# A state-space layer's vector work: GpSimd operations moved to VectorE or dropped, the lag matrix spread by DMA, one scan per unit, and the gated output fetched back from DRAM

## The chip, the cores and the metric

The kernel runs on one NeuronCore of a Trainium2 chip. The metric is the device time of one execution in microseconds; the number given for a kernel is the median of its runs, and lower is better. The engines are named as in the profile: PE is TensorE (PEld its weight loads), DVE is VectorE, ACT is ScalarE, POOL is GpSimd, SP is SyncE, which issues nearly all transfers here.

## The reference, cut to what matters

One inference step of a two-layer decoder: 1024 prompt tokens and 64 sample tokens (8 sequences of 8), width 1024. The change lies in the first mixer, a diagonal complex state-space layer (S5), and in the start of the gated linear unit behind it:

```python
lam_bar = exp(lam * dt)                       # 64 groups x 64 complex states
bu  = einsum('blgc,gpc->blgp', u, b_bar)      # 16 channels of a group -> 64 states
h   = pows * h_prev + associative_scan(lam_bar, bu)
y   = real(einsum('blgp,gcp->blgc', h, c)) + d_skip * u
z   = gelu(y)
gl  = z @ w_glu                               # 1024 -> 2048
out = gl[..., :1024] * sigmoid(gl[..., 1024:])
```

Everything is float32. Then follow a convolutional feed-forward layer, differential attention and a second feed-forward layer, which the change leaves as they are.

## The kernel before, in words

The kernel is written against a tile framework with a scheduler: the program is recorded in the order of the code, and the scheduler (`tile.TileContext(nc, schedule_with_timeline_sim=True)`) then sets the order of instructions on each engine. An engine runs its instructions strictly in that order, and so does SP's queue of DMA issues. Tiles come from pools with a fixed number of buffers per name; an instruction that writes a buffer waits until the readers of its last contents are done.

`s5()` handles 1024 tokens as 128 chunks of 8 steps (`NCH`=128, `L`=8). Inside a chunk the recurrence is a matrix product over 8 x 16 = 128 (step, channel) pairs; between chunks it is a scan along 128 chunk numbers. The 64 groups go in 8 blocks of 8 (`BG`=8), and each block in units of 3, 3 and 2 groups: 24 units.

For each block there are
- `angles(b)`: the tables `cosT`, `sinT` (128 x 1024) of the chunk rotation, by two POOL operations (L416, L419), one on DVE (L417) and four on ACT (L418 to L422);
- `block_in(b)`: loads the block's 128 channels of the prompt as `zk` (512 KB, L430, three buffers) and scales them into `xg` (eight ACT operations, L432);
- `tables(b)`: `gn` and `cl`, each a product on DVE (L458) plus a product `cw` on POOL (L459), added on DVE (L461); then `cw` becomes a copy of `cl` with its two halves of 64 partitions exchanged, by two 256 KB transfers (L463, L464). For block 0 the same in three pieces, all on DVE (L450 to L454).

For each unit
- `stage_t`: PE transposes `xg` into `U` and `gn` into `M2` (both evacuated by ACT); the lag matrix `M1` is a PE product of `gn` and `cl` (L490), to which DVE adds the skip gain on the diagonal, one instruction per group (L492), and POOL zeroes what lies above the block diagonal (L494);
- `stage_s`: PE product `M2`·`U`; DVE rotates it (`za` L509, `zb` in two halves because the halves are crossed L511, subtraction L512), adds the sample states (`Vs` L513), runs one scan per group (`E`, L519) and multiplies by the cosine (L522), POOL by the sine (L523) and forms the last state (`Wf` L521);
- `stage_y`: three PE products per group give y (L534 to L536) and two small ones the sample rows (L539, L541); ACT applies gelu into the `zk` buffer (L543) and, per group, into `zs` (L547).

After a block's last unit `stage_z(b)` transposes `zk` (8 times) and `zs` (8 times) on PE, and `split_evac` writes the pair `xT_hi` (ACT, L140) and `xT_lo` (DVE, L141), which the gated unit reads. The loop at L588 emits `stage_t` two units ahead, and `block(b)` and `angles(b)` piece by piece between units. The gated unit `glu()` first loads its weights as 256 KB `raw` pieces (`load_w`, L675; `whi` L680, `wlo` L681) and then runs three PE products per tile in the token order `ORDER_U`.

Of the kernel before, what the change touches and what calls it, by code (L numbers as in the profile page):

```python
# [10 lines left out]
F32 = mybir.dt.float32  # L11
# [62 lines left out]
def trunk_kernel(ctx, tc, I, O):  # L74
# [7 lines left out]
    def nm(s):  # L82
        uid[0] += 1
        return f"{s}_{uid[0]}"
# [19 lines left out]
    mmagic = ctile([P, 1], "mmagic")  # L104
    V.memset(mmagic, -MAGIC)
    sgn2pi = ctile([P, 1], "sgn2pi")
    V.memset(sgn2pi[0:64, :], -TWO_PI)
    V.memset(sgn2pi[64:128, :], TWO_PI)

    x1d = dpool.tile([T, D], F32, tag="x1d", name="x1d")  # L110

# [56 lines left out]
    def s5():  # L168
        with ExitStack() as c5:
# [17 lines left out]
            Ex = kt_([P, 4, G], "Ex")  # L187
# [3 lines left out]
            dgc = kt_([P, G], "dgc")  # L191
# [9 lines left out]
            with tc.tile_pool(name="s5prep", bufs=1, reuse_waits="tile") as pr:  # L201
# [165 lines left out]
                gx = pt([G, L, C], "gx")  # L367
                GP.tensor_copy(gx, bc(adn[:, 1], 1, L))
                PE.transpose(ps[:, 0:G], gx.rearrange("g j c -> g (j c)"), idg)
                A.copy(dgc, ps[:, 0:G])  # L370
# [8 lines left out]
                A.copy(Ex, ps[:, 0 : 4 * G].rearrange("p (w g) -> p w g", g=G))  # L379
# [23 lines left out]
            NBK = G // BG  # L403
            v4 = lambda t: t.rearrange("p g (j c) -> p g j c", c=C)
            trig = {}
            blocks = {}
            zs2 = bp.tile([2 * 32, L, P], F32, tag="zs", name="zs2", bufs=1)
# [4 lines left out]
            def angles(b):  # L412

                gs = slice(b * BG, (b + 1) * BG)
                cosT, sinT = bt_("cosT", 3), bt_("sinT", 3)
# [4 lines left out]
                A.activation(cosT, sinT, AF.Abs)  # L420
                A.activation(sinT, sinT, AF.Sin, scale=sgn2pi)
                A.activation(cosT, cosT, AF.Sin, bias=halfpi, scale=-TWO_PI)  # L422
                trig[b] = (cosT, sinT)

            def block_in(b):
                chs = slice(b * P, (b + 1) * P)
                xg = bt_("xg")
                zk = bp.tile([P, L, P], F32, tag="zk", name=nm("zk"), bufs=3)
                zs = zs2[32 * (b % 2) : 32 * (b % 2) + NB]
                nc.sync.dma_start(zk, xp[:, :, chs])  # L430
                for j in range(L):
                    A.mul(v4(xg)[:, :, j], zk[:, j].rearrange("p (g c) -> p g c", c=C), rs[:, j : j + 1])  # L432
                return xg, zk, zs

            def tables(b):
# [10 lines left out]
                if b == 0:  # L446
                    for u0 in range(0, BG, 3):
                        u = slice(u0, min(u0 + 3, BG))
                        for out, w in ((gn, 0), (cl, 2)):
                            V.tensor_tensor(v4(out)[:, u], yb(w)[:, u], tb(w)[:, u], ALU.mult)  # L450
                            V.tensor_tensor(v4(cw)[:, u], yb(w + 1)[:, u], tb(w + 1)[:, u], ALU.mult)
                            V.tensor_tensor(out[:, u], out[:, u], cw[:, u], ALU.add)
                        nc.sync.dma_start(cw[0:64, u], cl[64:128, u])
                        nc.sync.dma_start(cw[64:128, u], cl[0:64, u])  # L454
                        yield
                    return
                for out, w in ((gn, 0), (cl, 2)):
                    V.tensor_tensor(v4(out), yb(w), tb(w), ALU.mult)  # L458
                    GP.tensor_tensor(v4(cw), yb(w + 1), tb(w + 1), ALU.mult)  # L459
                    yield  # L460
                    V.tensor_tensor(out, out, cw, ALU.add)  # L461
                    yield
                nc.sync.dma_start(cw[0:64], cl[64:128])  # L463
                nc.sync.dma_start(cw[64:128], cl[0:64])  # L464
# [7 lines left out]
            def stage_t(k):  # L472
                b, u0, nu = units[k]
                xg, zk, zs, gn, cl, cw = blocks[b]
                g0 = b * BG + u0
                U = ut("U", NU, 3)
                ps = psum_u()
                for i in range(nu):
                    PE.transpose(ps[:, i * P : (i + 1) * P], xg[:, u0 + i], ident)
                A.copy(U[:, 0:nu, 0:NCH], ps[:, 0 : nu * P].rearrange("p (u k) -> p u k", k=P))  # L480
                GP.tensor_copy(U[:, 0:nu, NCH:NU], Us[:, g0 : g0 + nu])
                M2 = ut("M2", P, 2)
                ps = psum_m2()
                for i in range(nu):
                    PE.transpose(ps[:, i * P : (i + 1) * P], gn[:, u0 + i], ident)
                A.copy(M2[:, 0:nu], ps[:, 0 : nu * P].rearrange("p (u q) -> p u q", q=P))
                M1 = ut("M1", P, 3)
                ps = psum_m1()
                for i in range(nu):
                    PE.matmul(ps[:, i * P : (i + 1) * P], gn[:, u0 + i], cl[:, u0 + i], start=True, stop=True)  # L490
                for i in range(nu):
                    V.scalar_tensor_tensor(M1[:, i], ident, dgc[:, g0 + i : g0 + i + 1],  # L492
                                           ps[:, i * P : (i + 1) * P], op0=ALU.mult, op1=ALU.add)
# [1419 lines left out]
```

## Time and profile before

| | before |
|---|---|
| median of 3 runs | 2796.93 us (2788.64 to 2798.99) |
| profiled execution | 2793.4 us, span 2791.7 us |
| TensorE clock in it, mean | 0.959 |
| PE busy | 2527.1 us (91%) |
| DVE busy | 2034.1 us (73%) |
| ACT busy | 1264.8 us (45%) |
| POOL busy | 742.6 us (27%) |
| the stage `s5()` | from the start to about 291 us |

All three runs are within 0.4% of each other. The profiled execution is 3.5 us below the median. Busy shares over the whole span say little here, since the state-space stage is a tenth of the time and has other limits than the rest: rows restricted to a stretch of the span are read instead. In rows of a line's instructions the three durations are minimum, median and maximum in ns; in rows of groups come the summed busy time in us and the mean of one in ns. In the rows of the timeline the first number is the start, the second the time until the last of the xN instructions ends, and the bracket is idle time ahead and what ended it. "SPq" is the issue of a transfer on SP's queue, not its run.

### The profile page before, as it was taken

To read this page: it belongs to the slowest core of one execution; us is meant where nothing else is said; L and a number is where in the kernel's file an instruction comes from. 1 tells how busy PE (TensorE), PEld (TensorE's weight loads), DVE (VectorE), ACT (ScalarE), POOL (GpSimd) and SP (SyncE) were. 2 spreads that over 40 slices of the span, in tenths; PEclk is the share of its full clock that TensorE was granted. 3 is DMA by queue.
4 is the path that set the end of the run, shared out by engine and by line. 5 is a ranking of instruction groups with operands and counts; after the bars stand their busy time and mean duration, and the time that the engine had idled before them with its cause. 6 is when DMAs were issued, how large, how long until landed. Compare 5 with 4: busy or idle time off the path is not lost.

```text
span 2791.7 us, 39050 instructions
## 1 busy us (share of the span) xinstructions
PE 2527.1 (91%) x14162; PEld 2220.9 (80%) x14162; DVE 2034.1 (73%) x3828; ACT 1264.8 (45%) x2453; POOL 742.6 (27%) x998
## 2 busy tenths in 40 slices
PE   2657899799999999999999899999799999998996
PEld 2556688699999987777877688887599999996774
DVE  9999325877767779988232588884977777778998
ACT  5554212444444454336232377773544444444432
POOL 5665000021223237620120222210011111027661
PEclk9778999899999999999999899999899999999998
DMA  4110222212222233335455633324422222233334
GB/s 117 35 36 26 85 72 83 83 63 76 74 71 71 71 108 110 91 110 185 162 197 180 171 74 87 90 79 129 142 68 78 72 76 82 71 96 112 95 93 143
DMA packets 241557, 269.69 MB, mean 97 GB/s; under 512 B 28828, under 2 KB 191316, under 8 KB 241364
## 3 DMA queue, kind: packets, MB, share of 16 engines
q1 hardware_dynamic: 237044, 254.93, 29.5%
q0 software_dynamic: 3232, 10.29, 1.9%
q8 instruction: 112, 1.84, 0.3%
q10 hardware_dynamic: 1088, 1.97, 0.2%
q14 instruction: 81, 0.66, 0.1%
HBM read 187.03 MB, written 67.53 MB: 91 GB/s over the span
## 4 chain that ended last, share of the span: by engine, by line
PE 67%; DVE 20%; DMA 4%; issue 3%; ACT 3%; POOL 2%; SPq 0%; DVEq 0%; POOLq 0%; ACTq 0%
PE mm L697 19%; PE mm L698 19%; PE mm L699 19%; PE mm L1260 2%; DVE xT_lo L141 2%; DVE acc L1271 2%; DVE S L1733 1%; DMA gr<-gd 1%; DVE E L519 1%; PE tr L744 1%; ACT S L1737 1%; DVE zb L511 1%; PE mm L1761 1%; DVE gn L458 1%; DVE S L1747 1%
## 5 line engine op out<-in xcount | busy, mean ns | idle before, releaser
L697 PE MATMUL mm<-xT_hi,whi 128*128 128x320 f32 (+1 forms) x1408 | 458.4, 327 | 2.8 <-DVE acc L1015 1.3
L698 PE MATMUL mm<-xT_lo,whi 128*128 128x320 f32 (+1 forms) x1408 | 456.2, 324 | 0.1
L699 PE MATMUL mm<-xT_hi,wlo 128*128 128x384 f32 (+1 forms) x1408 | 453.3, 324 | 0.0
L1049 POOL COPY cvo<-acc 128x2 f32<-128x2 f32 x88 | 102.0, 1159 | 759.7 <-ACT acc L1032 759.7
L697 PEld LDWEIGHTS mm<-xT_hi,whi 128*128 128x128 f32 x1408 | 264.9, 189 | 8.3 <-DVE acc L1015 5.0
L698 PEld LDWEIGHTS mm<-xT_lo,whi 128*128 128x128 f32 x1408 | 265.6, 189 | 0.9 <-DVE xT_lo L141 0.9
L699 PEld LDWEIGHTS mm<-xT_hi,wlo 128*128 128x128 f32 x1408 | 265.1, 188 | 0.2
L1046 DVE SCALAR_TENSOR_TENSOR acc<-acc,cpar,acc 128x1104 f32<-128x1104 f32 x176 | 240.2, 1385 | 5.3 <-ACT acc L1044 5.2
L697 PE MATMUL mm<-whi,xT_hi 128*128 128x512 f32 x576 | 228.1, 402 | 5.7 <-ACT whi L680 5.7
L698 PE MATMUL mm<-wlo,xT_hi 128*128 128x512 f32 x576 | 228.3, 398 | 0.0
L699 PE MATMUL mm<-whi,xT_lo 128*128 128x512 f32 x576 | 227.8, 397 | 0.0
L141 DVE TENSOR_TENSOR wlo<-raw,whi 128x1024 fp32r<-128x1024 f32 x88 | 107.4, 1221 | 159.5 <-PE mm L698 153.7
L140 ACT CAST whi<-raw 128x1024 fp32r<-128x1024 f32 x88 | 92.5, 1051 | 285.9 <-PE mm L699 269.2
L1271 DVE TENSOR_TENSOR acc<-mm,acc 128x512 f32<-128x512 f32 x279 | 184.1, 678 | 11.0 <-PE mm L699 10.6
L697 PE MATMUL mm<-acc,whi 128*128 128x384 f32 x528 | 179.5, 340 | 4.2 <-DVE acc L1006 3.4
L698 PE MATMUL mm<-acc,whi 128*128 128x384 f32 x528 | 179.5, 340 | 0.0
L699 PE MATMUL mm<-acc,wlo 128*128 128x384 f32 x528 | 179.5, 340 | 0.0
L697 PEld LDWEIGHTS mm<-whi,xT_hi 128*128 128x128 f32 x576 | 108.9, 189 | 35.1 <-ACT whi L680 5.8
L699 PEld LDWEIGHTS mm<-whi,xT_lo 128*128 128x128 f32 x576 | 108.5, 188 | 26.4 <-issue 0.9
L698 PEld LDWEIGHTS mm<-wlo,xT_hi 128*128 128x128 f32 x576 | 108.5, 188 | 25.5 <-issue 0.4
L1733 DVE CUSTOM_DVE_ANT_0 S<-mm,tb 128x512 f32<-128x512 f32 (+3 forms) x192 | 101.4, 551 | 32.7 <-PE mm L1731 31.0
L1044 ACT ACTIVATE acc<-acc,cpar 128x1104 f32<-128x1104 f32 x88 | 113.9, 1311 | 19.8 <-DVE acc L1015 10.1
(548 smaller groups left out, 6448.9 us busy)
## 6 DMA issues: line engine op xcount, KB each, us to landing
raw<-in_w_up_dram SPq DMA_DIRECT2D x88, 512.0 KB
gd<-acc SPq DMA_DIRECT2D x44, 552.0 KB
raw<-in_w_down_dram SPq DMA_DIRECT2D x44, 512.0 KB
gr<-gd SPq DMA_DIRECT2D x80, 256.0 KB
raw<-in_glu_w_dram SPq DMA_DIRECT2D x32, 256.0 KB
acc<-in_cache_k_dram SPq DMA_DIRECT2D x16, 512.0 KB
acc<-in_cache_v_dram SPq DMA_DIRECT2D x16, 512.0 KB
xj<-in_x_prompt_dram SPq DMA_DIRECT2D x8, 512.0 KB
```

The costliest lines, as they stand in the source:

```text
L140: A.copy(hi_ap, ps_ap)
L141: V.tensor_tensor(lo_ap, ps_ap, hi_ap.bitcast(F32), ALU.subtract)
L458: V.tensor_tensor(v4(out), yb(w), tb(w), ALU.mult)
L697: PE.matmul(out, lh, rh, start=start, stop=False, **kw)
L698: PE.matmul(out, lh, rl, start=False, stop=False, **kw)
L699: PE.matmul(out, ll, rh, start=False, stop=stop, **kw)
L1044: A.activation(hc, hb[:, 2 : 2 + TG], AF.Identity, bias=cp[:, ft, 3:4], scale=cp[:, ft, 2:3])
L1046: V.scalar_tensor_tensor(hc, hb[:, tap : tap + TG], cp[:, ft, tap : tap + 1], hc, op0=ALU.mult, op1=ALU.add)
L1049: GP.tensor_copy(co[:, 0:2], hb[:, SEQ : SEQ + 2])
L1260: PE.matmul(pa[h], lt, wt[:, h * 512 : (h + 1) * 512], start=st and j == 0, stop=sp and j == len(seq) - 1)
L1271: V.tensor_tensor(a, ps, a, ALU.add)
L1733: V.tensor_tensor_reduce(S_[j][:, k0 : k0 + w], ps[:, 0:w], H["tb"][:, b0 : b0 + w], 0.125, -3e38, ALU.add, ALU.max, mx[:, j, c : c + 1])
```

## The change

- Angles: `angles(q)` serves two blocks. Half the partitions hold one block and half the other, so that three DVE operations (L427 to L429 of the changed kernel) and four on ACT make the tables of both; eight 256 KB transfers inside SBUF (L438) lay them out for the two blocks. POOL takes no part.
- Tables: the two products that POOL made are on DVE (L465). The extra table `sr` carries the sign, so that `stage_s` can add rather than subtract.
- Lag matrix: per block, eight small products with 16 weight columns give its first 16 rows (L475), four ACT copies bring them into a persistent buffer `M1s[b % 2]` (L478), one POOL product and one DVE addition put the skip gain on (L480, L481), and seven transfers copy shifted parts to the other seven 16-row bands (L483). The 64 DVE and 24 POOL operations of L492 and L494 go.
- Units: PE makes the product a second time with its halves crossed (`pw`, L524; `M2` gets 64 more columns by a second ACT copy, L509), so that `zb` is one DVE operation; the scans of a unit become one (L536) over 3 x 129 elements with a multiplier tile `R` that ACT fills (L511); the product with the sine is on DVE (L539), and `Wf` is a POOL copy.
- Output: `stage_y` applies one gelu to all sample rows of a unit (`zs`, one buffer) and sends them to a DRAM tensor `zsd`, one transfer per group with rows of 64 bytes (L568). `stage_z` sends `zk` (now two buffers) to the DRAM tensor `zd` (L575); only block 7 is still transposed from SBUF. In `glu()`, a new `split(tt)` loads 128 tokens by 896 channels back (L898), transposes them and splits them, one tile ahead of use.
- `block(bn)` is emitted whole, at the last unit of block bn-2.

```diff
-                GP.tensor_tensor(sinT, bc(Ex[:, 3, gs], 2, NCH), bc(kk, 1, BG), ALU.mult)
-                V.tensor_scalar(cosT, sinT, MAGIC, None, op0=ALU.add)
-                A.activation(cosT, cosT, AF.Identity, bias=mmagic)
-                GP.tensor_tensor(sinT, cosT, sinT, ALU.subtract)
...
+            def angles(q):
+                x, t, sr = [bt_(n, 1) for n in ("ax", "at", "as")]
+                V.tensor_tensor(x, bc(PH[:, q], 2, NCH), bc(kk, 1, BG), ALU.mult)
+                V.tensor_scalar(t, x, MAGIC, None, op0=ALU.add)
+                V.scalar_tensor_tensor(x, t, MAGIC, x, op0=ALU.subtract, op1=ALU.subtract)
+                A.activation(t, x, AF.Abs)
+                A.activation(sr, x, AF.Sin, scale=-TWO_PI)
+                A.activation(x, x, AF.Sin, scale=TWO_PI)
+                A.activation(t, t, AF.Sin, bias=halfpi, scale=-TWO_PI)
+                for h in range(2):
+                    i = slice(64 * h, 64 * h + 64)
+                    cosT, sinT = bt_("cosT", 3), bt_("sinT", 3)
+                    for dst, r, src in ((cosT, 0, t), (sinT, 0, sr), (cosT, 64, t), (sinT, 64, x)):
+                        nc.sync.dma_start(dst[r : r + 64], src[i])
...
-                zk = bp.tile([P, L, P], F32, tag="zk", name=nm("zk"), bufs=3)
+                zk = bp.tile([P, L, P], F32, tag="zk", name=nm("zk"))
...
-                    GP.tensor_tensor(v4(cw), yb(w + 1), tb(w + 1), ALU.mult)
+                        V.tensor_tensor(v4(cw)[:, u], yb(w + 1)[:, u], tb(w + 1)[:, u], ALU.mult)
...
+                M1 = M1s[b % 2]
+                ps = psum()
+                for g in range(BG):
+                    PE.matmul(ps[32 * (g % 4) : 32 * (g % 4) + C, g // 4 * P : (g // 4 + 1) * P], gn[:, g, 0:C],
+                              cl[:, g], start=True, stop=True, skip_group_check=True)
+                for i in range(4):
+                    A.copy(M1[0:C, i:BG:4], ps[32 * i : 32 * i + C, 0 : 2 * P].rearrange("p (a w) -> p a w", w=P))
+                dd = bp.tile([C, BG, C], F32, tag="dd", name=nm("dd"), bufs=1)
+                GP.tensor_tensor(dd, bc(ident[0:C, 0:C], 1, BG), bc(dT[:, gs], 2, C), ALU.mult)
+                V.tensor_tensor(M1[0:C, :, 0:C], M1[0:C, :, 0:C], dd, ALU.add)
+                for j in range(1, L):
+                    nc.sync.dma_start(M1[C * j : C * j + C, :, C * j : P], M1[0:C, :, 0 : P - C * j])
...
-                for o, i in ((slice(0, 64), slice(64, 128)), (slice(64, 128), slice(0, 64))):
-                    V.tensor_tensor(zb[o, 0:nu], s1[i, :, 0:NCH], sinT[i, us], ALU.mult)
-                V.tensor_tensor(za[:, 0:nu], za[:, 0:nu], zb[:, 0:nu], ALU.subtract)
+                V.tensor_tensor(zb[:, 0:nu], pw[:, 0 : nu * P].rearrange("p (u k) -> p u k", k=P), sinT[:, us], ALU.mult)
+                V.tensor_tensor(z, z, zb[:, 0:nu], ALU.add)
...
-                for i in range(nu):
-                    r8 = Ex[:, 0, g0 + i : g0 + i + 1].broadcast_to([P, NCH - 1])
-                    V.tensor_tensor_scan(E[:, i, 1:NCH], za[:, i, 0 : NCH - 1], r8, 0.0,
-                                         op0=ALU.add, op1=ALU.mult)
-                GP.tensor_tensor(zb[:, 0:nu], E[:, 0:nu], sinT[:, us], ALU.mult)
+                V.tensor_tensor_scan(f(E), f(za), f(R), 0.0, op0=ALU.add, op1=ALU.mult)
+                V.tensor_tensor(zb[:, 0:nu], E[:, 0:nu, 0:NCH], sinT[:, us], ALU.mult)
...
+                zs = up.tile([P, P], F32, tag="zs", name=nm("zs"), bufs=1)
+                A.activation(zs[0 : 32 * nu], pq[0 : 32 * nu], AF.Gelu_apprx_tanh)
                 for i in range(nu):
+                    nc.sync.dma_start(zsd.rearrange("(b t) (g c) -> g b t c", t=L, c=C)[g0 + i],
+                                      zs[32 * i : 32 * i + NB].rearrange("b (t c) -> b t c", c=C))
...
+                if b < NBK - 1:
+                    nc.sync.dma_start(zd.rearrange("(k j) d -> k j d", j=L)[:, :, b * P : (b + 1) * P], zk)
+                    return
...
+        def split(tt):
+            t0, n = tokens(tt)
+            y = slot("acc")
+            e = D if tt == NTT else D - P
+            nc.sync.dma_start(y[0:n, 0:e], zsd if tt == NTT else zd[t0 : t0 + n, 0:e])
+            for h in range(2):
+                m = min(4, e // P - 4 * h)
+                ks = slice(4 * h, 4 * h + m)
+                split_evac(xh[:, ks, t0 : t0 + n], xl[:, ks, t0 : t0 + n],
+                           transposed(y[0:n, 512 * h : 512 * h + m * P], n))
+
+        split(ORDER_U[0])
         ws = units(0)
```

The scheduler's order shows three places on which the prediction rests. Numbers at the end of names count buffers as they are handed out. First, DVE in one block in the middle of the stage, before:

```order
L461 TENSOR_TENSOR gn_1256<-gn_1256,cw_1258 128x1024
L141 TENSOR_TENSOR xT_lo<-mm_1220,xT_hi 128x4x128
L141 TENSOR_TENSOR xT_lo<-mm_1227,xT_hi 128x4x128
L141 TENSOR_TENSOR xT_lo<-mm_1234,xT_hi 128x8x8
L492 SCALAR_TENSOR_TENSOR M_198_1278<-ident,dgc,mm_1279 128x128 x2
L458 TENSOR_TENSOR gn_1492<-Yt,Dt 128x1024
L509 TENSOR_TENSOR za_1289<-mm_1285,cosT_879 128x384
L511 TENSOR_TENSOR zb_1290<-mm_1285,sinT_880 64x384 x2
L513 TENSOR_TENSOR Vs<-mm_1285,G_102 128x8x3
L522 TENSOR_TENSOR za_1191<-E_1198,cosT_879 128x384
L512 TENSOR_TENSOR za_1289<-za_1289,zb_1290 128x384
L461 TENSOR_TENSOR cl_1257<-cl_1257,cw_1258 128x1024
```

The same place in the changed kernel (M_37_453 is the persistent lag matrix `M1s[0]`, ax and at are the angles of the next pair of blocks):

```order
L539 TENSOR_TENSOR zb_1211<-E_1217,sinT_920 128x384
L464 TENSOR_TENSOR gn_1479<-Yt,Dt 128x1024
L427 TENSOR_TENSOR ax_1775<-PH,kk 128x1024
L467 TENSOR_TENSOR gn_1250<-gn_1250,cw_1252 128x1024
L428 TENSOR_SCALAR at_1776<-ax_1775 128x1024
L465 TENSOR_TENSOR cw_1252<-Yt,Dt 128x1024
L429 SCALAR_TENSOR_TENSOR ax_1775<-at_1776,ax_1775 128x1024
L467 TENSOR_TENSOR cl_1251<-cl_1251,cw_1252 128x1024
L529 TENSOR_TENSOR za_1305<-mm_1297,cosT_919 128x3x128
L532 TENSOR_TENSOR Vs<-mm_1297,G_99 128x8x3
L530 TENSOR_TENSOR zb_1306<-mm_1298,sinT_920 128x384
L481 TENSOR_TENSOR M_37_453<-M_37_453,dd_1274 16x8x16
```

Before, DVE spreads products, additions, the diagonal (L492) and the split evacuation (L141) between units. Now all six table operations of the next block stand behind the unit's scan, and the addition L481, which needs the ACT copies of that block's first lag rows, stands among the operations of the second unit.

Second, SP's queue over one block, before:

```order
L464 DMA cw_804<-cl_803 64x1024
L430 DMA zk_1246<-in_x_prompt_dram 128x8x128
L463 DMA cw_1040<-cl_1039 64x1024
L464 DMA cw_1040<-cl_1039 64x1024
L430 DMA zk_1482<-in_x_prompt_dram 128x8x128
```

and after (zk_1033 is the block that ends, zk_1469 the one that is fetched into its buffer):

```order
L568 DMA zsd<-zs_1334 64x1x16 x3
L438 DMA cosT_1785<-at_1776 64x1024
L438 DMA sinT_1786<-as_1777 64x1024
L568 DMA zsd<-zs_1411 64x1x16 x3
L438 DMA cosT_1785<-at_1776 64x1024
L575 DMA zd<-zk_1033 1024x1x128
L438 DMA sinT_1786<-ax_1775 64x1024
L568 DMA zsd<-zs_1463 64x1x16 x2
L445 DMA zk_1469<-in_x_prompt_dram 128x8x128
L469 DMA cw_1481<-cl_1480 64x1024
L470 DMA cw_1481<-cl_1480 64x1024
L483 DMA M_38_454<-M_38_454 16x8x112
```

A load of `zk` used to have only the previous exchange of `cw` ahead of it; it now stands behind the transfer of the finished block to `zd`, the sample rows and the angle tables. On ACT, the copies into the lag matrix follow the scaling of the freshly loaded block, and in this block the angles too. Before:

```order
L486 COPY M_297_1803<-tr_1804 128x384
L432 ACTIVATE xg_1935<-zk_1936,rs 128x8x16 x8
L420 ACTIVATE cosT_1787<-sinT_1788 128x1024
L480 COPY U_1796<-tr_1797 128x3x128
L543 ACTIVATE zk_1482<-mm_1758 128x3x8x16
L547 ACTIVATE zs_453<-mm_1758 8x8x16 x3
L421 ACT_TABLE_LOAD
```

After:

```order
L508 COPY M_202_1290<-tr_1291 128x2x128
L509 COPY M_202_1290<-tr_1291 128x2x64
L447 ACTIVATE xg_1239<-zk_1240,rs 128x8x16 x8
L430 ACTIVATE at_1776<-ax_1775 128x1024
L431 ACT_TABLE_LOAD
L431 ACTIVATE as_1777<-ax_1775 128x1024
L433 ACTIVATE at_1776<-at_1776,halfpi 128x1024
L432 ACTIVATE ax_1775<-ax_1775 128x1024
L478 COPY M_37_453<-mm_1261 16x2x128 x4
L508 COPY M_220_1368<-tr_1369 128x3x128
```

The copies M_37_453 can only run when the load of zk_1240 and four angle operations are through.

Third, SP's queue where the gated unit begins, before:

```order
L642 DMA out_ssm_re_sample_dram<-gs__2303 128x4x64
L642 DMA out_ssm_im_sample_dram<-gs__2303 128x4x64
L675 DMA raw_2365<-in_glu_w_dram 128x2x256 x2
L675 DMA raw_2372<-in_glu_w_dram 128x2x256
L1381 DMA gr_2323<-in_kv_norm_g_dram 128x8x1
L1381 DMA gr_2326<-in_b_pre_g_dram 128x8x1
L1387 DMA gr_2330<-in_lam_q_dram 128x64
L1388 DMA gr_2330<-in_lam_k_dram 128x64
L1387 DMA gr_2335<-in_lam_q_dram 128x64
```

After:

```order
L644 DMA out_ssm_re_sample_dram<-as_2253 128x4x64
L644 DMA out_ssm_im_sample_dram<-as_2253 128x4x64
L1401 DMA gr_2273<-in_kv_norm_g_dram 128x8x1
L1401 DMA gr_2276<-in_b_pre_g_dram 128x8x1
L1407 DMA gr_2280<-in_lam_q_dram 128x64
L1408 DMA gr_2280<-in_lam_k_dram 128x64
L1407 DMA gr_2285<-in_lam_q_dram 128x64
L1408 DMA gr_2285<-in_lam_k_dram 128x64
L1416 DMA gr_2312<-in_sub_g_dram 128x1
L898 DMA acc_2315<-zd 128x896
L677 DMA raw_2330<-in_glu_w_dram 128x2x256 x2
```

Three weight pieces used to leave before the small `gr` loads of the later attention; now all seven `gr` loads and the first piece of `zd` come first.

More of the change, by code (lines that the diff above doesn't have):

```diff
@@ L403, in s5 @@
             NBK = G // BG
+            NE = NCH + 1
             v4 = lambda t: t.rearrange("p g (j c) -> p g j c", c=C)
@@ L598, in s5 @@
                 for bn in range(1, NBK):
-                    at = k - 3 * (bn - 2)
-                    for _ in range(sum(x <= at for x in BST) if k == -LA else BST.count(at)):
-                        if bn not in steps:
-                            steps[bn] = block(bn)
-                        next(steps[bn], None)
-                if k >= 0 and units[k][1] == AT and units[k][0] + 2 < NBK:
-                    b = units[k][0]
-                    if b % 2 == 1:
-                        angles(b + 1)
-                        angles(b + 2)
+                    if k == max(-LA, 3 * bn - 4):
+                        for _ in block(bn):
+                            pass
+                if k >= 0 and units[k][1] == 0 and units[k][0] % 2 == 1 and units[k][0] + 2 < NBK:
+                    angles((units[k][0] + 1) // 2)
             ps = psum_t()
             PE.transpose(ps[0:G, 0:P], Wf, ident)
-            fs = up.tile([G, 2, S], F32, tag="fs", name="fs", bufs=1)
-            ft = up.tile([G, 2, S], F32, tag="ft", name="ft", bufs=1)
+            fs, ft = [bt_(n, 1)[0:G, 0:2, 0:S] for n in ("ax", "at")]
             wre = ps[0:G, 0:S]
@@ L902, in glu @@
                     ao[tt] = slot("acc")
-                ps = tok_mm(tt, ws, xsx)
+                    k = ORDER_U.index(tt) + 1
+                    if k < len(ORDER_U):
+                        split(ORDER_U[k])
+                    if tt == NTT:
+                        xsx = sample_pair()
+                ps = tok_mm(tt, ws, None if n == P else xsx)
                 if n < P:
```

169 lines of the change are left out of this document (72 added, 97 removed).

## The prediction, made before the changed kernel was run

> **What bounds the kernel now.** I first split the span by stage: busy time of each engine in three stretches.
>
> ```profile
> 60.00:280.00 220.00, 144.65 (x1083) 124.92 (x1081) 208.23 (x323) 120.13 (x240) 137.63 (x137) 0.80 0.12 32
> 280.00:300.00 20.00, 11.26 (x71) 9.45 (x72) 11.23 (x28) 6.39 (x14) 4.38 (x8) 0.71 0.29 60
> 300.00:420.00 120.00, 120.00 (x540) 96.42 (x539) 29.62 (x63) 23.81 (x37) 0.00 (x0) 0.99 0.26 81
> ```
>
> In the state-space stage DVE is busy 208 of 220 us and sets the pace; PE has 145, POOL 138. From 300 us on, in the gated unit, PE is busy without a gap. So DVE work counts up to 280, and every PE operation moved behind 300 costs its full length. The pace itself is the distance of the `zk` loads on SP's queue:
>
> ```profile
> 128.10 0.59 SPq L430 DMA_DIRECT2D zk<-in_x_prompt_dram  x1
> ...
> 219.73 0.59 SPq L430 DMA_DIRECT2D zk<-in_x_prompt_dram  x1
> ```
>
> There are two more between these, so a block takes (219.73 - 128.10)/3 = 30.5 us. Is DVE slow by itself? The timeline of DVE and POOL and the rows of single lines say no:
>
> ```profile
> 127.06 3.02 POOL L459 TENSOR_TENSOR cw<-Yt,Dt 128x1024 f32<-128x1024 f32 x1
> 127.56 2.93 DVE L512 TENSOR_TENSOR za<-za,zb 128x384 f32<-128x384 f32 x1
> ...
> 145.54 0.55 DVE L512 TENSOR_TENSOR za<-za,zb 128x384 f32<-128x384 f32 x1
> ```
> ```profile
> L512 DVE TENSOR_TENSOR za<-za,zb x24: 415/550/2930, 83.4 to 282.4; 128x384 f32<-128x384 f32 x16, 128x256 f32<-128x256 f32 x8
> L519 DVE TENSOR_TENSOR_SCAN E<-za,Ex x64: 388/396/2777, 84.3 to 283.2; 128x127 f32<-128x127 f32 x64
> L458 DVE TENSOR_TENSOR cl<-Yt,Dt x7: 1916/1994/2333, 56.4 to 249.6; 128x1024 f32<-128x1024 f32 x7
> L461 DVE TENSOR_TENSOR cl<-cl,cw x7: 1215/1217/3371, 72.4 to 260.0; 128x1024 f32<-128x1024 f32 x7
> L522 DVE TENSOR_TENSOR za<-E,cosT x24: 527/932/2401, 86.9 to 283.9; 128x384 f32<-128x384 f32 x16, 128x256 f32<-128x256 f32 x8
> L509 DVE TENSOR_TENSOR za<-mm,cosT x24: 396/543/554, 79.7 to 280.5; 128x384 f32<-128x384 f32 x16, 128x256 f32<-128x256 f32 x8
> L513 DVE TENSOR_TENSOR Vs<-mm,G x24: 175/183/190, 81.4 to 281.8; 128x24 f32<-128x24 f32 x16, 128x16 f32<-128x16 f32 x8
> L459 POOL TENSOR_TENSOR cw<-Yt,Dt x14: 2558/2861/3017, 46.5 to 255.3; 128x1024 f32<-128x1024 f32 x14
> ```
>
> The same subtraction takes 0.55 us alone and 2.93 while POOL's product runs, ending with it (130.1 against 130.5). L509, which reads one input from PSUM, never exceeds 0.554. So two-input operations on SBUF are held by POOL, and the change takes nearly all POOL work away.
>
> **The change, step by step.** *DVE's own work for a block.* A unit of three: `za` 0.54, `Vs` 0.18, `zb` 0.54 (one whole-width operation like L509 for two halves), addition 0.55, scan, cosine and sine 0.53 each. The one long scan is not in the trace. Three of the old take 3 x 0.388 = 1.16, the upper end; an addition of that width, 0.55, is the lower. Most of 0.388 must be per element, as 24 elements in L513 take 0.18 in all: 0.388 - 0.16 = 0.23 for 127, three times that and one fixed part give 0.85. Sum 3.7; these start-to-end times overlap by some 0.05 to 0.1 (127.06 to 130.41 shows it at L512), so 3.4. Two such units and one of two groups (2.5): 9.3. Tables: four products of 1.92 and two additions of 1.22 make 10.1, less overlap 9.6: POOL's products, 2.86 beside DVE, become 1.83 on it. Half of an angle set (three operations, 1.9 + 0.7 + 1.2) 1.7, the small addition L481 0.2. In all 20.8 us against 30.5. Gone are the 64 diagonal additions (2.7 us a block), `split_evac` of seven blocks, two extra `zb` halves.
>
> *The round that now ties blocks together.* Before, `zk` had three buffers and never left SBUF. Now two buffers must go to DRAM before the next block can be read into them. The rows for its legs, from SP, ACT and PE:
>
> ```profile
> 132.28 2.44 ACT L432 ACTIVATE xg<-zk,rs 128x128 f32<-128x128 f32 x8 [1.30 <-DMA zk<-in_x_prompt_dram]
> 147.77 0.59 SPq L464 DMA_DIRECT2D cw<-cl  x1
> 149.00:150.00 1.00, 1.00 0.98 221
> 151.00:152.00 1.00, 1.00 0.00 0
> 16.61 0.50 SPq L233 DMA_DIRECT2D xsd<-xs  x1
> 21.32 5.23 SPq L236 DMA_DIRECT2D zt<-xsd  x4
> L422 ACT ACTIVATE cosT<-cosT,halfpi 128x1024 f32<-128x1024 f32 x8 | 9.1, 1134 | 0.0
> L480 ACT COPY U<-tr 128x384 f32<-128x384 f32 (+1 forms) x21 | 9.3, 443 | 50.8 <-PE mm L539 50.8
> L535 PE MATMUL mm<-cl,za 128*128 128x128 f32 x118 | 29.1, 336 | 21.5 <-DVE za L522 21.5
> ```
>
> A 512 KB load takes 132.28 - 128.10 = 4.2 us from issue to first use. Two 256 KB copies run at 221 GB/s and are through by 151, 3.3 us after issue. A write to DRAM and back is seen once: `xsd` written at 16.61, read back from 21.32, an upper end of 4.7 for that leg; the lower is the copies' 3.3. I take 4.2 as for the read. The round: after L481, DVE makes the block's second and third unit, 3.4 + 2.5 = 5.9; six products and the gelu 2.2; write 4.2; read 4.2; eight scalings 2.4; four copies of 256 elements, 0.35 each, 1.4; L481 0.2. That is 20.5. On SP the transfer waits behind sample rows and angle copies: five issues of some 0.5, and half of the 1 MB of angle tables (1 MB at 221 GB/s is 4.7) is 2.4: 4.9 together, of which I count 4, because some leave while gelu runs. In two of six rounds the angles (three sines of 1.13, one table load) stand ahead of the four copies on ACT, some 4.7: 1.5 on average. Sum 26.0, above DVE's 20.8: DVE waits 5 us a block, the queue behind it with it, and this round is late next. So 26.0 for 30.5.
>
> The Trainium skill, "DMA: Bandwidth & Descriptors", section "Anatomy of one DMA — SWDGE (gpsimd) path", fits 2.0 us fixed plus bytes/436 GB/s, mostly the receipt of the write, heaviest for HBM; for 512 KB that is an estimate of 3.2 a leg. The row has 4.2 for the read on SP's queue, so I keep it; by the page the sum would be 2 us a round or 12 us less.
>
> *Start and end.* Before the first unit:
>
> ```profile
> 43.05 1.00 DVE L450 TENSOR_TENSOR gn<-Yt,Dt 128x384 f32<-128x384 f32 x1 [0.22 <-PE mm L385]
> ...
> 64.46 8.00 DVE L452 TENSOR_TENSOR cl<-cl,cw 128x384 f32<-128x384 f32 x3
> 72.38 3.37 DVE L461 TENSOR_TENSOR cl<-cl,cw 128x1024 f32<-128x1024 f32 x1
> ...
> 79.74 0.54 DVE L509 TENSOR_TENSOR za<-mm,cosT 128x384 f32<-128x384 f32 x1
> ```
>
> Three additions took 8.00 under POOL's angles. Now block 0's tables (as many elements as any block's, 9.6), block 1's 9.6 and the first angles 3.4 put the unit at 43.05 + 22.6 = 65.7; add 4 for PE's and ACT's share behind `cl` (before, 79.74 - 75.75 = 4.0): 70, 10 us earlier. Block 0 takes 17 (its units, the angles of the next pair, one product), six rounds 156, block 7 to its last unit 7: last `za` at 250. I add 3 for some 30 handovers of 0.1: 253 against 280.5, 27 us earlier.
>
> *The gated unit.*
>
> ```profile
> 290.41 0.40 SPq L642 DMA_DIRECT2D out_ssm_re_sample_dram<-gs__2303  x1
> 290.72 1.10 PE L561 MATMUL mm<-ident,zk 128*128 128x128 f32 x8 [0.48 <-ACT zk L543]
> 291.41 1.58 SPq L675 DMA_DIRECT2D raw<-in_glu_w_dram  x3
> 293.03 1.97 SPq L1381 DMA_DIRECT2D gr<-in_kv_norm_g_dram  x1
> 298.15 2.50 PE L697 MATMUL mm<-whi,xT_hi 128*128 128x512 f32 x5 [5.74 <-ACT whi L680]
> 299.39 1.46 SPq L675 DMA_DIRECT2D raw<-in_glu_w_dram  x3
> ```
>
> The last `za` begins at 280.5 (the row of L509 above), the first product 17.65 us later, 298.15 - 291.41 = 6.7 of it from the issue of the first weights. Now the `gr` loads stand ahead of them, 299.39 - 293.03 = 6.4 us, as does 448 KB of `zd`, 2.1 at 221 GB/s: 8.5, so the first product is 18.5 earlier. Then PE, full to 420, gets 64 transposes of 1.10/8 = 0.14: 8.8. The first tiles also wait for `zd` behind the weights, between 0 and the 5.74 of this row, I take 3. Net -18.5 + 8.8 + 3 = -6.7. The split evacuations hide in the idle DVE and ACT there (29.6 and 23.8 of 120). What follows has the same instructions: nothing. 2793.4 - 6.7 = 2786.7 against this profiled execution, which lies 3.5 under the median: between that and 2790 I say 2788. About 0.5%, 14 us, is what a measurement tells from no change.
>
> **The rivals.** *DVE alone sets the pace.* If write, read and queue fit beside the other units, the round is below 20.8. For it: DMA share 0.12 in this stage. Against: `zk` has two buffers, so nothing lets the load start earlier. It gives up to 6 x 5.2 = 31 us more: 2757. *The round trip is longer than the old pace* (the other side). The legs start from 64-byte pieces of `zsd` (`zt`, also 64 bytes, took 5.23/4 = 1.3 us of SP each) and 512-byte pieces of `zd`. With 1.1 us more on each of four serial pieces (write, read, the queue ahead of each) the round is 30.5 and the last `za` where it was, and the gated unit's start costs 8.5 + 8.8 + 3 = 20: 2815. The kernel is slower than before from +0.3 each, and by over 0.5% from +1.0. The Trainium skill, "DMA: Bandwidth & Descriptors", in the section named above, speaks for this one, as it calls the receipt of a write to HBM the heaviest; no row here times it apart. *PE at half clock.* The clock is 0.80 here; if DVE's waits drop it to half, PE's 144.65/220 x 30.5 = 20 us a block become up to 27, about 1 more than the round: 2794. *The change does not free DVE:* should DVE's long operations be held by something else than POOL, it keeps some 28.5 us a block, 6 x 2.5 = 15 more than forecast: 2803.
>
> **Chances.** Forecast (round 25 to 28 us, 2774 to 2800) 0.47; DVE alone 0.22; long round trip 0.22; half clock 0.05; not freed 0.04. Faster by over 0.5%, below 2783: the second and a third of the first, 0.38. Slower, above 2811: nearly all of the third, 0.21. Within: the rest, 0.41. For eight in ten: down to 2760, short of the full gain of the second, up to 2816, short of the worst of the third.
>
> **What would show it.** Right: DVE's two-input operations all near their minimum; the long scan near 0.85; `zk` loads 26 us apart; DVE idle some 5 us before L481, released by ACT's copies; first `za` near 70, last near 253; first gated product near 280. Wrong: L481 never waited for, with loads 21 us apart; loads 30 apart, with ACT waiting for `zk` over 5 us after its issue; PE gaps of more than 6 us in the gated unit's first 20; or `za` at full length beside idle POOL.

## The result, and the profile after

The changed kernel took 2822.18 us (median of 4 runs, 2819.52 to 2823.95) against 2793.62 us for the kernel before (now the median of 4 runs): ratio 1.0101, 95% interval 1.0077 to 1.0125. It is 1% slower. The forecast was 2788 us, slightly faster than before, with a range of 2760 to 2816; the time lies above that range, and "slower by over 0.5%" had a chance of 0.21. The profiled execution has a span of 2822.2 us against 2791.7, so 30.5 us are to be explained.

The same three stretches as before, now of the changed kernel (busy time of PE, PEld, DVE, ACT, POOL, then clock, DMA share, GB/s):

```profile
60.00:280.00 220.00, 129.44 (x1149) 113.77 (x1147) 159.98 (x243) 94.42 (x238) 38.85 (x78) 0.78 0.43 100
280.00:300.00 20.00, 11.23 (x39) 8.13 (x40) 10.33 (x30) 6.21 (x10) 0.00 (x0) 0.67 0.67 219
300.00:420.00 120.00, 111.31 (x507) 87.86 (x507) 28.64 (x50) 25.67 (x45) 0.00 (x0) 0.96 0.25 77
```

DVE went from 208 to 160 us of 220, POOL from 138 to 39. So the stage has the slack that the change was to make, and no other engine has become as busy: PE is at 129, ACT at 94. In the gated unit PE, which had been busy for all of 300 to 420, now idles for 9 us of it.

The starts of the same instructions in each kernel, read from the rows of their lines, tell in which stage the time goes. All times in us from the start of the span; "gated" is the first gated product, "w_up" the first load of the feed-forward weights, "x2d", "x3d" and "y" the first stores of the first feed-forward layer, of the attention layer and of the result. The kernels e1 to e10 are the experiments below.

| | first za | last za | gated | w_up | x2d | x3d | y | span |
|---|---|---|---|---|---|---|---|---|
| before | 79.7 | 280.5 | 298.1 | 447.9 | 1256.1 | 1956.8 | 2758.7 | 2791.7 |
| after | 68.7 | 265.0 | 288.7 | 462.5 | 1270.3 | 1977.9 | 2790.0 | 2822.2 |
| e1 | 68.8 | 265.3 | 288.6 | 462.8 | 1266.9 | 1961.1 | 2762.1 | 2794.4 |
| e2 | 68.7 | 276.2 | 298.6 | 451.5 | 1259.7 | 1956.8 | 2768.6 | 2801.7 |
| e3 | 68.7 | 271.8 | 294.1 | 446.7 | 1253.2 | 1951.7 | 2753.0 | 2785.2 |
| e4 | 73.1 | 282.4 | 298.7 | 447.9 | 1257.1 | 1956.2 | 2757.2 | 2790.0 |
| e5 | 68.8 | 262.8 | 286.1 | 460.1 | 1265.1 | 1964.7 | 2765.5 | 2798.4 |
| e6 | 68.8 | 263.0 | 282.6 | 453.1 | 1263.3 | 1959.7 | 2771.8 | 2803.5 |
| e7 | 68.9 | 252.5 | 276.1 | 450.0 | 1255.9 | 1955.1 | 2767.1 | 2799.5 |
| e8 | 68.9 | 249.1 | 266.8 | 419.7 | 1228.1 | 1921.2 | 2722.1 | 2755.6 |
| e9 | 69.1 | 249.7 | 269.9 | 440.6 | 1249.4 | 1943.8 | 2755.8 | 2788.4 |
| e10 | 68.8 | 267.5 | 285.1 | 438.3 | 1249.5 | 1946.8 | 2748.9 | 2781.5 |

After against before: the first gated product 9.4 us earlier; from there to w_up 173.8 us against 149.8, 24.0 lost, so w_up is 14.6 later; the first feed-forward layer 0.4 gained; from x2d to x3d 707.6 against 700.7, 6.9 lost; from x3d to y 812.1 against 801.9, 10.2 lost; 0.8 gained at the end. The sum is 30.5. Half of the loss lies in stages whose code is the same line for line. A few us in one stage mean little: the first feed-forward layer up to its first store (w_up to x2d), takes 804.1 to 809.2 us in the eight kernels in which nothing of it was changed (before, after, e1 to e5, e7).

DVE's own operations came out close to what was priced. Lines of the changed kernel, ns minimum, median, maximum:

```profile
L531 DVE TENSOR_TENSOR za<-za,zb x24: 425/549/561, 72.4 to 265.9; 128x384 f32<-128x384 f32 x16, 128x256 f32<-128x256 f32 x8
L536 DVE TENSOR_TENSOR_SCAN E<-za,R x24: 694/964/984, 75.2 to 266.4; 128x387 f32<-128x387 f32 x16, 128x258 f32<-128x258 f32 x8
L464 DVE TENSOR_TENSOR cl<-Yt,Dt x10: 596/1926/1950, 45.4 to 237.3; 128x1024 f32<-128x1024 f32 x7, 128x384 f32<-128x384 f32 x2, 128x256 f32<-128x256 f32 x1
L467 DVE TENSOR_TENSOR cl<-cl,cw x10: 438/1220/1240, 63.5 to 243.3; 128x1024 f32<-128x1024 f32 x7, 128x384 f32<-128x384 f32 x2, 128x256 f32<-128x256 f32 x1
```

The addition that had reached 2.93 us never exceeds 0.561 with POOL quiet. The Trainium skill, "GPSIMD Engine Reference", section "1. Specifications", says that GpSimd shares its SBUF interfaces with VectorE and contends with DVE instructions that have two SBUF inputs; these rows agree. The long scan takes 0.96 us (0.85 was assumed, within its bounds of 0.55 and 1.16).

What the engines wait for now is read from the chain of work that ended last, here over one block of the changed kernel:

```profile
154.02 4.29 DMA zd<-zk
158.38 3.99 DMA zk<-in_x_prompt_dram
162.43 0.26 issue
162.70 2.15 ACT xg L447 x7
164.89 0.90 PE tr L499 x3
...
167.07 0.99 PE mm L475 x16
168.06 1.66 PE mm L522 x6
169.72 1.08 PE mm L524 x6
```

The write of the finished block, the read of the next into the same buffer, its scaling, then PE: this is the round that the prediction named, and its legs are 4.3 and 4.0 us where 4.2 each was taken. The fit in the Trainium skill, "DMA: Bandwidth & Descriptors", section "Anatomy of one DMA — SWDGE (gpsimd) path", had given an estimate of 3.2 a leg; on SP's queue, with these pieces, the measurement decides. Whether the write leg itself holds the pace is not settled by the chain; e3, e9 and e10 below bear on it. The waits of DVE and ACT (engine, line, what it waited for: us in all, times, longest) between 70 and 265 us:

```profile
DVE za L529 <- PE mm L522: 21.7, 12, 4.6
DVE M L481 <- ACT M L478: 16.8, 6, 5.8
...
ACT xg L447 <- DMA zk<-in_x_prompt_dram: 46.3, 6, 9.9
ACT R L511 <- DVE E L536: 25.1, 11, 4.1
ACT zs L566 <- DMA zsd<-zs: 18.3, 10, 3.7
```

The forecast had all of DVE's waiting, 5 us a block, ahead of L481. Over the six rounds it is 2.8 a block there and 3.6 at the first rotation `za`, which waits for PE.

The loads of `zk` on SP's queue:

```profile
102.88 0.61 SPq L445 DMA_DIRECT2D zk<-in_x_prompt_dram  x1
...
158.38 0.61 SPq L445 DMA_DIRECT2D zk<-in_x_prompt_dram  x1
...
238.91 0.63 SPq L445 DMA_DIRECT2D zk<-in_x_prompt_dram  x1
```

There are three more: five distances in 136.0 us, 27.2 us a block against 30.5 before and 26.0 forecast.

### The profile page after: what moved, and what is told of

It is laid out like the page before. It is cut to its first block, busy times and chain, and to the rows that moved or that the text cites. A ratio compares the mean times of both kernels' runs of the same rounds, so it can differ in the third digit from the quotient of the medians.

```text
span 2822.2 us, 39388 instructions
## 1 busy us (share of the span) xinstructions
PE 2522.9 (89%) x14234; PEld 2210.1 (78%) x14234; DVE 1976.6 (70%) x3743; ACT 1248.3 (44%) x2470; POOL 691.0 (24%) x933
## 4 chain that ended last, share of the span: by engine, by line
PE 66%; DVE 17%; DMA 5%; issue 4%; ACT 4%; POOL 3%; SPq 1%; DVEq 0%; POOLq 0%; ACTq 0%
PE mm L699 18%; PE mm L700 18%; PE mm L701 18%; DVE acc L1291 2%; PE mm L1280 2%; DVE xT_lo L138 2%; DVE S L1753 1%; DMA gr<-gd 1%; PE tr L747 1%; POOL xr L1172 1%; DMA raw<-in_w_down_dram 1%; DVE xT_hi L138 1%; ACT S L1757 1%; DVE wst L138 1%; DVE cw L465 1%
## 5 line engine op out<-in xcount | busy, mean ns | idle before, releaser
L1069 POOL COPY cvo<-acc 128x2 f32<-128x2 f32 x88 | 158.5, 1801 | 673.5 <-ACT acc L1052 673.5
L700 PEld LDWEIGHTS mm<-wlo,xT_hi 128*128 128x128 f32 x576 | 109.0, 189 | 26.9 <-DVE wlo L683 1.5
```

What stands on the lines that cost most here:

```text
L700: PE.matmul(out, lh, rl, start=False, stop=False, **kw)
L1069: GP.tensor_copy(co[:, 0:2], hb[:, SEQ : SEQ + 2])
```

## The experiments

The theory after this reading had three parts: the round holds the state-space stage at 27 us a block; reading `zd` back costs the gated unit over 20 us; the later stages lose time to something that the change disturbs without touching it. The rivals are in the expectations.

**e1: the late loss.** POOL at the attention's start, changed kernel:

```profile
1570.46 0.88 POOL L1664 DMA_DIRECT2D kr<-kd  x1 [0.18 <-PE mm L701]
1590.22 0.88 POOL L1648 DMA_DIRECT2D v<-vd  x1 [18.88 <-DMA od<-acc]
```

Before, the same issue had waited 6.78 us, for a product of PE. Where tiles of one kind rotate through buffers, the scheduler picks the buffer. In the changed kernel it seems to have put the tile that holds the sample attention's results on a buffer whose end lies under the first head's values `v0`; the addresses are in no row here. What the rows show is that `v0` was not loaded until 16 small transfers out of that tile were done:

```profile
1576.68 11.44 SPq L1552 DMA_DIRECT2D od<-acc  x16
```

The edit:

```diff
+            spare = slot("acc")
+            GP.memset(spare[:, 0:1], 0.0)
             c1, *obs = cut(slot("acc"), TS, *[2 * VD] * 4)
+            V.tensor_copy(c1[:, 0:1], spare[:, 0:1])
```

> The changed kernel, with one spare buffer taken just before the tile that holds the sample attention's results, so that this tile gets another place and head 0's values v0 no longer lie on it. Theory (the late loss at the attention's start comes from that overlap, not from the state-space stage): POOL issues v<-vd some 12 us earlier against its neighbours, the wait of 18.9 us for od<-acc goes, PE's wait for qwh falls from 14.9 to about 3 us, and the end comes 5 to 11 us earlier (2811 to 2817). Rival (the attention starts late for another reason, such as an engine order): no change, 2822.

Measured: 2798.97 us, ratio to before 1.0028 (1.0013 to 1.0043), 23 us under the changed kernel where 5 to 11 were expected. Everything up to w_up is within 0.3 us of it, and the same row now reads

```profile
1571.09 0.88 POOL L1651 DMA_DIRECT2D v<-vd  x1 [3.07 <-PE mm L1542]
```

PE's wait for `qwh` fell from 14.9 to 1.2 us. From x2d to x3d the kernel needs 694.2 instead of 707.6, from x3d to y 801.0 instead of 812.1. The first 13 us go with the wait; the kernels without it need 693 to 701 there, so its price is some 7 to 14 us. The 11 us of the second feed-forward layer do not go with it: e2 and e7 do not wait for these transfers and need 812 as well, while before, e3, e4, e5, e8 and e10 need 801 to 802. (e6 and e9, which also need 812, still wait 7.8 and 7.1 us for them, with the spare buffer in place.) So that layer has one of two lengths from kernel to kernel. In the changed kernel PE is busy 3.9 us longer in it than in e1 and idle 7.2 us longer, and one of POOL's rows in that layer differs, here in the kernel before (801.9 us) and then in the changed one (812.1 us):

```profile
L1049 POOL COPY cvo<-acc x44: 184/665/1007, 2046.5 to 2509.9; 128x2 f32<-128x2 f32 x44
...
L1069 POOL COPY cvo<-acc x44: 184/1234/3627, 2068.0 to 2528.1; 128x2 f32<-128x2 f32 x44
```

These copies take 1.78 to 1.80 us on average in all five kernels of 812 us and 0.54 to 0.67 in all seven of 801 to 802. Whether they make the layer long or only go with another order of its instructions was not tested, so the cause of this part stays open.

**e2 and e3: the output by way of DRAM.** e2 puts the transposes from `zk` back and reads nothing in the gated unit, e3 drops the write to `zd` too:

```diff
-        split(ORDER_U[0])
...
-                    if k < len(ORDER_U):
-                        split(ORDER_U[k])
+                    if k < len(ORDER_U) and ORDER_U[k] == NTT:
+                        split(NTT)
```

> The changed kernel, but every block is also transposed on PE from zk as before, so the gated unit reads nothing back; the transfer of zk to zd stays (nobody reads it). It separates the gated unit's start from the state-space stage. Theory (64 transposes and waits for zd cost 24 us between the first gated product and the first load of w_up): that stretch falls from 174 to about 150 us; the state-space stage keeps its 27 us a block, perhaps 1 to 2 more for the transposes and the split evacuations; the end comes 15 to 25 us earlier, about 2800, and up to 11 more if the attention's buffers also fall otherwise. Rival (the gated unit is slow because of its weights' order on SP): the stretch stays above 165 us.

Measured: 2805.22 us. From the first gated product to w_up 152.9 instead of 173.8: reading back costs 20.9 of the 24.0. In PE's rows of the changed kernel this is 64 transposes, of which those behind the first product take

```profile
L747 PE MATMUL tr<-ident,acc 128*128 128x128 f32 (+1 forms) x57 | 8.8, 303 | 6.3 <-DMA acc<-zd 6.3
```

8.8 us, one wait of 6.3 for a `zd` piece that stood behind eight weight loads on SP, and smaller waits, among them 2.3 us for weights and 1.0 for the split evacuations. In the whole stretch PE is idle 10.5 us, against none before and 0.6 in e2. The large wait begins 17 us after the first product:

```profile
311.87 2.58 PE L747 MATMUL tr<-ident,acc 128*128 128x128 f32 x11 [6.28 <-DMA acc<-zd]
```

The other 3.1 of the 24.0 us stay in e2, e3, e8 and e10 (152.6 to 153.2 us), which all still read the sample rows back from `zsd`; they were not taken apart. But the last `za` came 11 us later than without the edit (276.2 against 265.0).

> As the previous one, without the transfer of zk to zd: the prompt's z never leaves SBUF, zk keeps two buffers, only the sample rows go by DRAM. Theory (the round gelu, write 4.4, read 4.0, scaling, copies sets the block's 27 us): transposes and split evacuation (about 2.5 us) take the write's place, the loads of zk come about 25 us apart, 6 x 2 = 10 to 15 us less than the previous run, about 2787. Rival (DVE or PE, not the round, sets the pace): the same distance of 27 us and the same time as the previous run.

Measured: 2790.76 us, ratio to before 0.9998 (0.9985 to 1.0011). The time is near the theory's 2787, but not for its reason. Of the 16.5 us of span under e2, 10.5 lie in the second feed-forward layer, which has its long form in e2 and its short one here, and only 4.4 are there at the last `za`. The loads of `zk` came 28.9 us apart, not 25 (98.66 to 243.01), against 29.0 in e2: the rival had that right. Compared with the changed kernel the write is gone and evacuations stand in ACT's and DVE's orders in its place; ACT now waited longer for the sample rows' single buffer:

```profile
ACT zs L566 <- DMA zsd<-zs: 28.5, 12, 4.4
ACT M L478 <- PE mm L475: 16.4, 5, 3.3
```

**e4: POOL's work on DVE, nothing else.** The kernel before, with `GP.tensor_tensor` replaced by `V.tensor_tensor` in the angles, the products `cw` and the product with the sine.

> The kernel before, with only POOL's large two-input operations moved to DVE (the angles' product and difference, the products cw, the product with the sine); everything else as before. Theory (DVE's operations were stretched by POOL's, so taking POOL away frees about as much DVE time as the moved work costs): tables 9.6, units 14, angles 3.7, split 2.2 us a block make 29 to 30 against 30.5, DVE's operations all at their minimum, the end within 10 us of before, 2783 to 2795. Rival (the stretching costs DVE more than the work itself): loads of zk 27 us apart or less, below 2775. Other rival (it costs less): above 2805.

Measured: 2792.62 us, ratio 1.0 (0.9989 to 1.0011). The time is as the theory had it: the stage is full of DVE work either way, stretched or real. The loads of `zk` are 31.4 us apart, a little more than the 29 to 30 expected.

```profile
60.00:280.00 220.00, 139.57 (x1073) 121.28 (x1074) 205.19 (x365) 117.65 (x235) 53.20 (x89) 0.77 0.13 33
L522 DVE TENSOR_TENSOR za<-E,cosT x24: 413/554/572, 81.8 to 286.4; 128x384 f32<-128x384 f32 x16, 128x256 f32<-128x256 f32 x8
```

(the stretch and the product with the cosine, which had a median of 0.932 beside POOL). The slack that the change made came from the shorter units and the lag matrix, not from the move alone.

**e5 to e7: the links of the round, one at a time,** each on top of e1. e5: `zs` with two buffers, `E` with one. e6: `lam_column(cpool)` after `glu()`. e7: the lag matrix's part of `tables(b)` as a function of its own, called one unit later:

```diff
                         for _ in block(bn):
                             pass
+                    if k == 3 * bn - 3:
+                        lag(bn)
```

> The kernel of e1_spare_buffer with two buffers for the sample rows zs (and one instead of two for E, whose readers are on DVE itself and one POOL copy). Theory (the gelu into zs waits for the transfers of the unit before, 13.6 us of ACT between 100 and 240 us, and all that ACT does later in order, the scaling of zk among it, is late by that): the wait falls below 3 us, zk loads 1 to 2 us closer than 27.2, last za 6 to 12 us earlier than 265. Rival (the round write, read, scaling, copies sets the pace and the wait at zs lies inside it): the wait goes, the distance of the loads and the last za stay within 2 us.

Measured: 2800.19 us in its one run, last `za` 2.5 us earlier than in e1 (262.8 against 265.3), loads 26.9 us apart instead of 27.2. ACT's wait for `zsd` went from 18.3 to nothing and turned into a longer wait for the load (59.7 instead of 46.3 us). The rival is nearer: most of that wait lay inside the round.

> The kernel of e1_spare_buffer with the seven small gr loads and their DVE work recorded behind the gated unit rather than ahead of it. Theory (they cost SP's queue 4 to 6 us ahead of the first weights and zd): the first gated product comes 4 to 6 us earlier than 288.6, and so does the end of the gated unit, at 2790 to 2796 in all. Rival (the first product waits for zd's last piece or the transposes, not for SP): under 2 us earlier.

Measured: first gated product at 282.6, 6.0 earlier, and w_up at 453.1, 9.7 earlier. 2.3 of the 6.0 came already at the last `za`, for a reason that was not traced, so 3.7 are what the `gr` loads cost behind it. The long form of the second feed-forward layer took the gain back (2805.29 us in its one run, where 2790 to 2796 was expected).

> The kernel of e1_spare_buffer with the lag matrix of a block (its products, four ACT copies, the addition L481 and the transfers) recorded one unit later. Theory (DVE stands 14 us between 100 and 240 us before L481 for the ACT copies, which stand behind the scaling of a block that has just come from DRAM): that wait falls below 4 us and the block's distance to 25 us or less, last za 8 to 15 us earlier than 265. Rival (the round trip of zk holds the next unit's products anyway): the wait moves to za L529, behind PE's product of the new block, and the distance stays at 27.

Measured: last `za` at 252.5, 12.8 earlier, loads 25.7 apart, first gated product 12.5 earlier than in e1; again the long second layer (2801.30 us in one run). DVE's waits between 70 and 252:

```profile
DVE za L532 <- PE mm L525: 29.8, 10, 6.0
DVE M L484 <- ACT M L481: 3.9, 2, 2.7
```

The wait for the copies went from 16.8 to 3.9 us, and 8 of these 13 us came back at `za`. Both sides were partly right, the theory more.

**e8 to e10: all of it together,** with z kept in SBUF; then each of two parts taken out again.

> All of these at once, and the prompt's z kept in SBUF as in e3_no_dram: no zd, two zs buffers, lag matrix one unit later, gr loads late, spare buffer. Theory (each removes a link of the same chain; DVE, at 21 us a block with the split evacuations 23, then sets the pace): loads of zk 23 to 25 us apart, last za near 245 to 255, first gated product near 270, gated unit as before; 2760 to 2772. Rival (the load of zk after the last gelu, the scaling and the products are enough to hold 26 us): last za 265 or later, 2780 to 2790.

Measured: 2757.16 us (2752.03 to 2757.92), ratio to before 0.9878, 95% interval 0.9861 to 0.9895: faster than both kernels and than the 2760 to 2772 expected. Last `za` 249.1, loads 24.7 us apart, DVE's largest wait down from 21.7 to

```profile
DVE za L532 <- PE mm L525: 14.0, 7, 3.8
```

> The kernel of e8_together with the output by way of DRAM put back (zk to zd, read back in the gated unit), all else of e8 kept. Theory (the output by DRAM costs by itself: in the state-space stage the write of some 4.4 us in each round, in the gated unit 64 transposes and waits): from the first gated product to the first load of w_up 165 to 175 us against 153 in e8, first gated product 0 to 8 us later than 266.8, the end 15 to 30 us later than e8. Rival (its cost lay in what stood around it, the lag matrix and the gr loads, and is hidden once these are moved): within 8 us of e8.

Measured: 2792.43 us, 35 us over e8 where 15 to 30 were expected. The first gated product is 3.1 us later than in e8, the stretch to w_up 170.7 against 152.9: 20.9 at w_up. The rest of the 33 us of span lies in later stages, 11 of it in the long form of the second layer (812.0 against 800.9). The output by DRAM costs 21 us by itself up to w_up, but not where the theory put its first half. The last `za` is only 0.6 us later, and the loads of `zk`, first and last of six, in e8 and then in e9, are the same 24.7 us apart:

```profile
98.80 0.61 SPq L445 DMA_DIRECT2D zk<-in_x_prompt_dram  x1
222.33 0.62 SPq L445 DMA_DIRECT2D zk<-in_x_prompt_dram  x1
...
102.94 0.90 SPq L445 DMA_DIRECT2D zk<-in_x_prompt_dram  x1
226.57 0.63 SPq L445 DMA_DIRECT2D zk<-in_x_prompt_dram  x1
```

So the write in each round, in place of the transposes, costs the state-space stage next to nothing; 17.8 of the 20.9 us are paid in the gated unit.

> The kernel of e8_together with the lag matrix of a block made where the changed kernel makes it, one unit earlier. Theory (the copies into the lag matrix and DVE's wait for them are the largest single link, 13 us in e7): last za 8 to 14 us later than 249.1, first gated product by as much later than 266.8. Rival (once z stays in SBUF and zs has two buffers the wait is short): within 4 us of 249.1.

Measured: 2786.57 us, ratio to before 0.9989 (0.9978 to 1.0001); last `za` 18.4 later than in e8 and first gated product 18.3 later, more than the 8 to 14 expected. The loads are 27.8 us apart again, though nothing is written to DRAM. The place of the lag matrix is the largest single link of the state-space stage among those that were moved.

## Why the prediction was wrong, point by point

- *DVE freed from POOL:* right, operation by operation (only the long scan is longer, 0.96 against 0.85), as was the start (first `za` 68.7, forecast 70).
- *The round replaces DVE as the pace:* right in kind, not in every link. 27.2 us a block against 26.0 is 6 us over five distances. The legs of write and read had the forecast length, but the write is not what holds the pace: e8 and e9 have the same 24.7 us without it and with it, and e3 and e10 have 28.9 and 27.8 without it, with the transposes in its place, against 27.2. What the runs show is the other link of the sum, the copies into the lag matrix behind the scaling and DVE's wait for them: moved one unit later they give 12.8 us (e7 against e1), moved back they cost 18.4 (e10 against e8). The two rounds with angles on ACT ahead of the copies (30.15 and 29.54 us) are 4.4 longer than the other three (25.45 on average), as priced at 4.7. Mis-sized is the stretch from the scaling to the next unit ("four copies of 256 elements, 0.35 each, 1.4; L481 0.2"): behind the scaling PE first has to transpose the new block and make its products, which the sum left out there and the chain shows (164.89 on). The last `za` came at 265.0 instead of 253: the other 6 us of these 12 lie outside the five distances, in the first block and the last.
- *Start of the gated unit:* last `za` to first product 23.7 us, forecast 26.2. The `gr` loads cost 3.7 to 6.0 (e6), forecast 6.4. This term was 2.5 too high. Together with the last `za`, the first product came 9.4 us earlier than before instead of 18.5.
- *Inside the gated unit:* the transposes at 8.8 were right (57 of the 64 stand behind the first product); the 3 us for waits were not. The stretch lost 24.0 instead of 11.8. The bound of 5.74 was taken from a wait for weights; the single wait for `zd`, 6.3, passed it, which the prediction had named as a sign of being wrong, and PE was idle 10.5 us in all. The remaining 4.7 us are products that took longer in sum, the sample rows' among them; they were not taken apart.
- *"What follows has the same instructions: nothing":* this step failed most, by 16 us. The instructions are the same, their buffers and order need not be. Of these 16, the attention's 6.9 are shown by e1, where the wait is gone and the stage gets 13 us back. The second layer's 10.2 are one of its two lengths, 801 or 812 over twelve kernels, and why the changed kernel has the long one stays open.
- Together: 9.1 + 12.2 + 15.9 = 37.2 us above the forecast change of -6.7, which is the measured +30.5.
- *The rivals:* the long round trip was forecast to give 2815 and sits nearest to the time, but not for its reason: the legs were not longer. "DVE alone sets the pace" did not come true even in e8, where the loads are 24.7 us apart against 22.1 of DVE work in its rows, split evacuations included. "The change does not free DVE" is refuted by the additions, which never exceed 0.561 us. Nor did the clock drop to half: the stage has 0.78 after and 0.80 before. (The sum of that rival was off by itself: 20 us at a clock of 0.80 are 32 at half clock, not 27.)

## What to carry to other kernels

Here, once an engine was freed, the next limit was not another busy engine but a chain of waits through several: sum such a chain with every engine on it, PE included, and look where a waiting instruction stands in the order of an engine that others need. A link that is long in the trace need not be the one that holds the pace; take it out before believing it, as e9 against e8 and e10 against e8 do for the write and for the lag matrix. Sending an intermediate result to DRAM and back cost 21 us here, 18 of them at the consumer, where PE was already full. Where a scheduler sets orders and buffers, no later stage is "the same": compare the starts of stages between kernels before explaining a total, and give the range some width for it (here 16 us of 30).

## What the runs showed of the hardware and was not expected

A transfer of 64 pieces of 64 bytes holds SP's queue a little longer than one of 512 KB. All transfers of `zsd` (minimum, median, maximum in ns), and in the timeline six of them with their waits beside the write of a whole block:

```profile
L568 SPq DMA_DIRECT2D zsd<-zs x64: 663/696/1459, 87.1 to 273.3; - x64
...
227.57 6.32 SPq L568 DMA_DIRECT2D zsd<-zs  x6
235.60 0.59 SPq L575 DMA_DIRECT2D zd<-zk  x1
```

0.696 us each against 0.59: the eight of a block take 5.6 us of SP's queue, of the 27 that a block lasts, for 4 KB a transfer. The prediction had taken some 0.5 an issue.
